# A hybrid attention and RWKV-7 layer: input tiles in rings of four, gated outputs stored as split halves, and the first pair's sums of squares emitted later

## The chip, the cores and the metric

The kernel runs on one core of a Trainium2 chip. The metric is the time of one launch in device microseconds, from three runs. The core has a matrix engine (TensorE, PE in the profile), a vector engine (VectorE, DVE), a scalar engine (ScalarE, ACT), GpSimd (POOL) and a synchronisation engine (SyncE, SP) from whose queue nearly all transfers are issued. Each engine works through its own list of instructions in order; an instruction that needs another engine's result, or a buffer that is still being read, waits for it at the head of its list, and everything behind it on that engine waits too.

## The reference

One layer over a sequence of 256 frames of width 4096. A combined projection feeds sixteen heads of forgetting attention (FoX), 32 heads of an RWKV-7 scan and a SiLU gate; the gated outputs go through an output projection and a layer norm.

```python
proj = jnp.einsum('bsd,dc->bsc', x, w_in)
fox_cols, rw_cols, z = ...
...
fox_out = _fox_attention(fq, fk, fv, log_f)
...
rw = rw + (rw_prev - rw) * mu_shift
r, kr, vr, wd, ad = jnp.split(rw, ...)
w_raw = -jax.nn.softplus(-(w0 + jnp.tanh(wd) @ w_up)) - 0.5
decay = jnp.exp(-jnp.exp(w_raw))
a = jax.nn.sigmoid(a0 + ad @ a_up)
kk = (kr * k_k).reshape(hs)
kk = kk / jnp.maximum(jnp.linalg.norm(kk, axis=-1, keepdims=True), 1e-12)
kr = kr * (1.0 + (a - 1.0) * k_a)
y = _rwkv7_scan(rh, decay, kh, vh, -kk, kk * ah)
y = groupnorm(y) * gn_gain + gn_bias
bonus = jnp.sum(rh * kh * r_k, axis=-1, keepdims=True) * vh
rwkv_out = y + bonus
h = jnp.concatenate([fox_out, rwkv_out], axis=-1) * jax.nn.silu(z)
out = jnp.einsum('bsc,cd->bsd', h, w_out)
x = _layernorm(ALPHA * x + out, ln_gain, ln_bias, LN_EPS)
```

## The kernel before, in words

**Precision.** Every large product is made from split operands. A tile is copied to a rounded type (hi), and the rest, the tile minus hi, is a second tile of that type (lo). ScalarE makes hi (the copies in lines 139, 160 and 744) and VectorE lo (the subtractions in lines 140, 161 and 745). A product is then three matmuls: x hi by w hi (L145), x lo by w hi (L146) and x hi by w lo (L147).

**The prelude.** The 32 k-tiles of the activations (128 x 256 each) come in 17 pieces, two single ones and then pairs. For each piece three transfers are issued: the activations (xr, L112), the narrow LoRA columns (lr, L115; the first three from ScalarE's queue) and the first block's weights (wr, L118, a ring of four). Each xr and each lr has a buffer of its own. Then, per piece, the x tiles are split into x0 to x31, which stay in memory through the projection, lr is split and multiplied (accl), and wr is split and multiplied (acc).

**The main loop.** Eight pairs n of head groups by four blocks b of 512 columns by sixteen weight pieces q. `weights` hands out the next split piece and `fetch` (L216) issues the load of a later one into the ring of four raw buffers, followed by its split, whose hi and lo tiles have three buffers each. A piece is twelve matmuls of 128 x 512. In the timelines w_9h, w_9l are the halves of piece 9 of some block; with a program's numbers w2_0_11l is pair 2, block 0, piece 11. Between the matmuls `slot` advances generators that emit the rest of the work a step at a time: `ahead` (the LoRA products lp and `prepare`, for the head groups i), `chain` (`rwkv` for the pairs), `fox` (attention per head) and `unload`. A `wait(n)` in a generator lets n such steps pass; the table W holds the counts. A compile-time scheduler with a model of durations then sets the order on each engine, so that a changed line can move neighbours too.

**prepare(i)** makes the keys of head group i and, in the tile shl (hi and lo halves of 128 x 512), squares and products whose sums over each head come from two matmuls np with a matrix of ones (L446, L447), `W["np"]`, 6, steps after shl. VectorE goes on from np with n2, a reciprocal, ae and BK.

**rwkv(n)** runs the scan of pair n in chunks. It makes T by way of memory (td, T), transposes T into X on VectorE (L542), and forms qt (L548), Q, xp (L569) from them on TensorE. At its end the group norm runs on the pair's post tile: vs on TensorE, a square root on ScalarE (L626, with a table load ahead of it), a reciprocal (L627), two products and sums (L628, L629), and the gate.

**gate(y, key, k)** (L346) makes h = 0.5 y sz on VectorE (L349), 128 x 256. There are 32 such tiles, two attention and two RWKV ones per pair. Those with k below 28 ("far", the first seven pairs) are stored to the DRAM tensor hd (L351, 128 KB each); the last four stay in memory.

**The reload.** While the last block of the last pair runs, `get_h` (L738) brings the far tiles back for the output projection: `load_h` issues hin from hd, up to three ahead in a ring of three (L735), and get_h splits hin into the buffers of the x tiles, tile h_k in that of x_k, which TensorE must have read for the last time. The output projection (L765 to L767) multiplies the h tiles with the pieces of w_o (wo0_0 and on, from the same stream and ring as the weights), and the layer norm follows.

Of the kernel before, what the change touches and what calls it, by code (L numbers as in the profile page):

```python
# [10 lines left out]
F32 = mybir.dt.float32  # L11
BF16 = mybir.dt.bfloat16
F32R = mybir.dt.float32r
AF = mybir.ActivationFunctionType
ALU = mybir.AluOpType
AX = mybir.AxisListType

P = 128
S = 256
D = 4096  # L20
KT = D // P
G = 16
# [14 lines left out]
INNER = 14  # L37
# [4 lines left out]
W = {"fo": 3, "vs": 2, "np": 6, "gp": 5, "tp": 4, "d1": 8, "d2": 12, "xp": 3, "fs": 4, "fp": 5}  # L42
# [15 lines left out]
LW = 2 * LORA + NF  # L58
# [23 lines left out]
def layer(ctx: ExitStack, tc: tile.TileContext, xt, xtok, w_lora, w_main, w_o, up, par, mulora, fbias, lng, lnb, cst, out):  # L82
    nc = tc.nc
# [3 lines left out]
    dram = ctx.enter_context(tc.tile_pool(name="dram", bufs=1, space=bass.MemoryType.DRAM))  # L87
# [12 lines left out]
    spool = early.enter_context(tc.tile_pool(name="spool", bufs=1))  # L100
# [7 lines left out]
    l_raw = []  # L108
    w_raw = []
    for n, (k0, k1) in enumerate(pieces):  # L110
        raw = spool.tile([P, (k1 - k0) * S], F32, tag=f"xr{n}", name=f"xr{n}")
        nc.sync.dma_start(out=raw, in_=xt[:, k0:k1, :].rearrange("p k t -> p (k t)"))  # L112
        x_raw.append(raw)
        raw = spool.tile([P, (k1 - k0) * LW], F32, tag=f"lr{n}", name=f"lr{n}")
        (nc.scalar if n < 3 else nc.sync).dma_start(out=raw, in_=w_lora[:, k0:k1, :].rearrange("p k c -> p (k c)"))  # L115
        l_raw.append(raw)
        raw = wpool.tile([P, 1024], F32, tag="wr", name=f"wr{n}", bufs=4)
        nc.sync.dma_start(out=raw[:, : (k1 - k0) * OB], in_=w_main[0, 0][:, k0:k1, :].rearrange("p k c -> p (k c)"))  # L118
        w_raw.append(raw)
# [12 lines left out]
    def column(name, i):  # L132
        return prm[:, PAR.index(name), i : i + 1]
# [22 lines left out]
    for n, (k0, k1) in enumerate(pieces):  # L156
        for k in range(k0, k1):
            t = xpool.tile([P, 2, S], F32R, tag=f"x{k}", name=f"x{k}")
# [31 lines left out]
    def wait(n):  # L190
        for _ in range(n):
            yield
# [4 lines left out]
    def slot():  # L197
        for g in list(sides):
            try:
                next(g)  # L200
            except StopIteration:
                sides.remove(g)
# [42 lines left out]
    rp = mid.enter_context(tc.tile_pool(name="rp", bufs=1))  # L245
# [9 lines left out]
    def rt(name):  # L255
        return t256("t", name, 5)
# [18 lines left out]
    lr = const.tile([LORA, 2, 2, S], F32R, name="lr")  # L275
# [58 lines left out]

    hs = {}
    szs = {}
    hd = dram.tile([2 * G, P, S], F32, name="hd")

    def silu2(z, key):
        th = t256("zt", key + "t")  # L340
# [5 lines left out]
    def gate(y, key, k):  # L346
        far = k < 2 * INNER
        h = rp.tile([P, S], F32, tag="h" if far else f"h{k}", name=f"h{k}", bufs=2 if far else 1)
        nc.vector.scalar_tensor_tensor(h, y, 0.5, szs[key], ALU.mult, ALU.mult)  # L349
        if far:  # L350
            nc.sync.dma_start(out=hd[k], in_=h)  # L351
        hs[k] = h

    HALF = [slice(0, C), slice(C, P)]
# [1 line left out]
    def ch(t):  # L356
        return t.rearrange("p (c t) -> p c t", t=C)

    def flat(t):
        return t.rearrange("p a b -> p (a b)")  # L360
# [13 lines left out]
    def front(i):  # L374
        upt = ups[i]
        uph = rp.tile([LORA, 2, P], F32R, tag="uph", name=f"uph{i}")
        nc.scalar.copy(flat(uph), flat(upt))
        upl = rp.tile([LORA, 2, P], F32R, tag="upl", name=f"upl{i}")
        nc.vector.tensor_tensor(flat(upl), flat(upt), flat(uph).bitcast(F32), ALU.subtract)
        load_up(i + 1)  # L380
        yield
        lp = pst(f"lp{i}")
        for j in range(2):
            o = lp[:, j * S : (j + 1) * S]
            nc.tensor.matmul(o, uph[:, j, :], lr[:, j, 0, :], start=True, stop=False)
            nc.tensor.matmul(o, uph[:, j, :], lr[:, j, 1, :], start=False, stop=False)
            nc.tensor.matmul(o, upl[:, j, :], lr[:, j, 0, :], start=False, stop=True)
        tw = rt(f"tw{i}")
        nc.scalar.activation(tw, lp[:, :S], AF.Tanh, scale=0.5, bias=half[:, 0, i : i + 1])
        ta = rt(f"ta{i}")  # L390
        nc.scalar.activation(ta, lp[:, S:], AF.Tanh, scale=0.5, bias=half[:, 1, i : i + 1])
        yield
        nc.vector.tensor_scalar(tw, tw, -0.5 * DECAY, -0.5 * DECAY, ALU.mult, ALU.add)
        L = rt(f"L{i}")
        nc.vector.tensor_tensor_scan(L, cs[:, C_SCAN : C_SCAN + S], tw, 0.0, ALU.mult, ALU.add)
        eL = rp.tile([P, NCH, C + 1], F32, tag="eL", name=f"eL{i}")
        nc.gpsimd.memset(eL[:, :, 0:1], 1.0)
        nc.scalar.activation(eL[:, :, 1:], ch(L), AF.Exp)
        eI = t256("eI", f"eI{i}")
        nc.scalar.activation(eI, L, AF.Exp, scale=-1.0)  # L400
        yield
        am = t256("am", f"am{i}")
        nc.scalar.activation(am, ta, AF.Identity, scale=hka[:, 0, i : i + 1], bias=hka[:, 1, i : i + 1])
        ae = t256("ae", f"ae{i}")
        nc.vector.scalar_tensor_tensor(ae, ta, 1.0, eI, ALU.add, ALU.mult)
        return eL, eI, am, ae
# [3 lines left out]
    def prepare(i):  # L410
        n, u = divmod(i, 2)
        while u == 0 and n and n - 1 not in done:
            yield
        eL, eI, am, ae = yield from front(i)
        while (i, 1) not in rk:
            yield
        r, kr = rk[i, 0], rk[i, 1]
        if u == 0:
            pairs[n] = dict(
                lc=rp.tile([P, 2, NCH], F32, tag="lc", name=f"lc{n}"),  # L420
                BK=rp.tile([P, 2, NCH, P], F32, tag="BK", name=f"BK{n}"),
                lt=[rp.tile([P, 2, NCH, P], F32, tag=f"lt{j}", name=f"lt{j}_{n}") for j in range(2)],
                bon=rp.tile([P, 2, S], F32, tag="bon", name=f"bon{n}"),
            )
        q = pairs[n]
        k = rt(f"k{i}")
        nc.vector.tensor_tensor(k, kr, am, ALU.mult)
        sb = rp.tile([P, 2, S], F32, tag="Nb", name=f"sb{i}")
        nc.scalar.activation(sb[:, 0, :], kr, AF.Square, scale=column("k_k", i))
        nc.vector.scalar_tensor_tensor(sb[:, 1, :], r, column("r_k", i), k, ALU.mult, ALU.mult)  # L430
        shl = rp.tile([P, 2, 2, S], F32R, tag="shl", name=f"shl{i}")
        sh, sl = flat(shl[:, 0]), flat(shl[:, 1])
        nc.scalar.copy(sh, flat(sb))
        nc.vector.tensor_tensor(sl, flat(sb), sh.bitcast(F32), ALU.subtract)
        BK = q["BK"][:, u]
        lt = [q["lt"][j][:, u] for j in range(2)]
        nc.scalar.copy(q["lc"][:, u, :], eL[:, :, C])
        nc.vector.scalar_tensor_tensor(lt[0][:, :, 0:C], ch(kr), nkk[:, i : i + 1], eL[:, :, 0:C], ALU.mult, ALU.mult)
        nc.vector.tensor_tensor(lt[0][:, :, C:P], ch(r), eL[:, :, 1:], ALU.mult)
        nc.scalar.copy(lt[1][HALF[1]], lt[0][HALF[1]])  # L440
        for j in range(2):
            h = HALF[j]
            nc.vector.tensor_tensor(BK[h, :, KB[j][1]], ch(k)[h], ch(eI)[h], ALU.mult)
        yield from wait(W["np"])
        nps = pst(f"np{i}")
        nc.tensor.matmul(nps, onesr, sl, start=True, stop=False)  # L446
        nc.tensor.matmul(nps, onesr, sh, start=False, stop=True)  # L447
        n2 = rt(f"n2{i}")
        nc.vector.tensor_scalar(n2, nps[:, :S], 1e-24, None, ALU.max)
        nc.scalar.copy(q["bon"][:, u, :], nps[:, S:])  # L450
        nc.vector.reciprocal(n2, n2)
        nc.vector.scalar_tensor_tensor(ae, ae, 0.5, n2, ALU.mult, ALU.mult)
        for j in range(2):
            h = HALF[j]
            nc.vector.scalar_tensor_tensor(BK[h, :, KB[j][0]], ch(kr)[h], column("k_k", i)[h], ch(ae)[h], ALU.mult, ALU.mult)
        prepared.add(i)
# [267 lines left out]

    ht = {}

    hin = {}

    def load_h(k):
        if k in hin or k >= 2 * INNER:  # L730
            return
        while k not in hs:
            slot()
        hin[k] = rp.tile([P, S], F32, tag="hin", name=f"hin{k}", bufs=3)
        nc.sync.dma_start(out=hin[k], in_=hd[k])  # L735

    def get_h(k):
        for n in range(k, min(k + 3, 2 * INNER)):  # L738
            load_h(n)
        while k not in hs:  # L740
            slot()
        src = hin.get(k, hs[k])
        t = xpool.tile([P, 2, S], F32R, tag=f"x{k}", name=f"h{k}")
        nc.scalar.copy(t[:, 0, :], src)
        nc.vector.tensor_tensor(t[:, 1, :], src, t[:, 0, :].bitcast(F32), ALU.subtract)
        ht[k] = t

    def load_tok(b):
# [59 lines left out]
    for b, q in outs:  # L808
        if q == 0:
            pool, tag = (ps, "ps") if b == 1 or b and b % 2 == 0 else (pp, "pp")  # L810
# [3 lines left out]
        for j in range(2):  # L814
            k = 2 * q + j
# [138 lines left out]
```

## Time and profile before

| what | us |
|---|---|
| median of three runs | 1998.69 |
| lowest and highest run | 1998.67 and 2004.73 |
| the profiled execution's own time | 2001.74 |
| its span, first to last instruction | 1999.9 |
| TensorE busy in the span | 1977.0 |
| VectorE busy | 1331.2 |
| ScalarE busy | 1001.4 |

The span lies inside the profiled execution's time, and that execution was 3.05 us longer than the median run. The mean clock granted to TensorE was 0.993 of full speed. A row of a timeline gives the start, the duration, the engine, the line and operation, and in brackets how long the engine sat idle before it and what released it. A row of windows gives, for each stretch, the busy microseconds of TensorE, its weight loads, VectorE, ScalarE and GpSimd with the number of instructions, then TensorE's clock, the busy share of the DMA engines and the rate in GB/s.

### The profile page before, as it was taken

The numbers are of one execution on the slowest core, as the hardware profiler recorded it, in microseconds if no ns is written. First come the engines' busy times: TensorE is split into PE (matmuls) and PEld (weight loads), VectorE is DVE, ScalarE is ACT, GpSimd is POOL, SyncE is SP. The second block draws the span as 40 slices with busy tenths as digits, with TensorE's granted clock in tenths as the row PEclk, the third lists the DMA queues.
The fourth block names the chain that finished last, engine by engine and source line by source line (L and its number), as shares of the span: only waits on it lengthen the run. The fifth ranks groups of instructions, "written<-read, shape, count | busy, mean of one in ns | idle before, by whom it ended". The sixth has DMA issues, their size and how long they took to land.

```text
span 1999.9 us, 28369 instructions
## 1 busy us (share of the span) xinstructions
PE 1977.0 (99%) x10624; PEld 1619.1 (81%) x10624; DVE 1331.2 (67%) x2067; ACT 1001.4 (50%) x1506; POOL 34.8 (2%) x82
## 2 busy tenths in 40 slices
PE   8999999999999999999999999999999999999998
PEld 6878888888888888888888887888788878888885
DVE  5578567856785677567757685768576856655555
ACT  5554464456544654465446544644564555433332
POOL 0000000000000000000000000000000000000000
PEclk9999999999999999999999999999999999999998
DMA  8456556655665556555655665566556657866564
GB/s 289 142 187 194 181 169 198 187 188 164 191 194 177 175 180 194 182 181 179 199 172 182 184 206 159 178 194 199 161 170 208 215 182 233 270 192 192 186 201 157
DMA packets 140138, 379.74 MB, mean 190 GB/s; under 512 B 32168, under 2 KB 49592, under 8 KB 140000
## 3 DMA queue, kind: packets, MB, share of 16 engines
q1 hardware_dynamic: 139568, 377.50, 59.7%
q8 instruction: 83, 1.36, 0.3%
q10 hardware_dynamic: 432, 0.43, 0.1%
q14 instruction: 55, 0.45, 0.1%
HBM read 367.89 MB, written 9.98 MB: 189 GB/s over the span
## 4 chain that ended last, share of the span: by engine, by line
PE 92%; DMA 1%; DVE 1%; ACT 0%; SPq 0%; issue 0%; DVEq 0%; ACTq 0%
PE acc L145 22%; PE acc L147 22%; PE acc L146 22%; PE oacc L765 6%; PE oacc L767 6%; PE oacc L766 6%; PE tr L704 1%; PE yp L610 1%; PE gp L470 1%; PE up L585 1%; PE rh L558 1%; DMA hin<-hd 1%; PE sp L594 0%; PE vp L479 0%; DVE res L881 0%; PE tp L515 0%
## 5 line engine op out<-in xcount | busy, mean ns | idle before, releaser
L526 DVE TENSOR_TENSOR prod<-Nb,xc 128x8 f32<-128x8 f32 (+30 forms) x248 | 72.5, 292 | 7.7
L529 DVE TENSOR_REDUCE xc<-prod 128x8 f32<-128x16 f32 (+30 forms) x248 | 73.1, 295 | 6.0
L140 DVE TENSOR_TENSOR w_9l<-w,w_9h 128x1024 fp32r<-128x1024 f32 x31 | 37.9, 1223 | 51.9 <-ACT w_9h L139 50.1
L140 DVE TENSOR_TENSOR w_3l<-w,w_3h 128x1024 fp32r<-128x1024 f32 x31 | 37.9, 1224 | 36.7 <-ACT w_3h L139 36.7
L140 DVE TENSOR_TENSOR w_0l<-w,w_0h 128x1024 fp32r<-128x1024 f32 x31 | 37.9, 1223 | 32.9 <-ACT w_0h L139 32.9
L140 DVE TENSOR_TENSOR w_2l<-w,w_2h 128x1024 fp32r<-128x1024 f32 x31 | 37.9, 1223 | 32.1 <-ACT w_2h L139 32.1
L140 DVE TENSOR_TENSOR w_15l<-w,w_15h 128x1024 fp32r<-128x1024 f32 x31 | 37.9, 1224 | 31.7 <-ACT w_15h L139 31.7
L140 DVE TENSOR_TENSOR w_10l<-w,w_10h 128x1024 fp32r<-128x1024 f32 x31 | 37.9, 1224 | 30.9 <-ACT w_10h L139 30.9
L139 ACT CAST w_15h<-w 128x1024 fp32r<-128x1024 f32 x31 | 32.7, 1055 | 50.9 <-PE acc L146 49.6
L139 ACT CAST w_1h<-w 128x1024 fp32r<-128x1024 f32 x31 | 32.7, 1055 | 49.9 <-PE acc L146 49.9
L139 ACT CAST w_0h<-w 128x1024 fp32r<-128x1024 f32 x31 | 32.7, 1055 | 49.9 <-PE acc L146 49.9
L140 DVE TENSOR_TENSOR w_11l<-w,w_11h 128x1024 fp32r<-128x1024 f32 x31 | 37.6, 1212 | 28.5 <-ACT w_11h L139 28.5
L139 ACT CAST w_14h<-w 128x1024 fp32r<-128x1024 f32 x31 | 32.7, 1055 | 46.8 <-PE acc L146 45.0
L140 DVE TENSOR_TENSOR w_14l<-w,w_14h 128x1024 fp32r<-128x1024 f32 x31 | 37.9, 1223 | 26.8 <-ACT w_14h L139 26.8
L139 ACT CAST w_11h<-w 128x1024 fp32r<-128x1024 f32 x31 | 32.7, 1055 | 45.9 <-PE acc L146 43.8
L140 DVE TENSOR_TENSOR w_1l<-w,w_1h 128x1024 fp32r<-128x1024 f32 x31 | 37.9, 1222 | 22.6 <-ACT w_1h L139 22.4
L145 PE MATMUL acc<-w_4h,x 128*128 128x512 f32 x124 | 53.0, 427 | 0.0
L139 ACT CAST w_13h<-w 128x1024 fp32r<-128x1024 f32 x31 | 32.7, 1055 | 38.4 <-PE acc L146 26.7
L145 PE MATMUL acc<-w_6h,x 128*128 128x512 f32 x124 | 51.2, 413 | 0.0
L145 PE MATMUL acc<-w_1h,x 128*128 128x512 f32 x124 | 51.2, 413 | 0.0
L145 PE MATMUL acc<-w_2h,x 128*128 128x512 f32 x124 | 51.0, 411 | 0.0
L145 PE MATMUL acc<-w_5h,x 128*128 128x512 f32 x124 | 50.0, 403 | 0.0
(800 smaller groups left out, 6538.2 us busy)
## 6 DMA issues: line engine op xcount, KB each, us to landing
w<-in_w_main_dram SPq DMA_DIRECT2D x496, 512.0 KB, 3.5
wo<-in_w_o_dram SPq DMA_DIRECT2D x128, 512.0 KB, 3.5
Nb<-nd SPq DMA_DIRECT2D x16, 512.0 KB, 5.1
wr<-in_w_main_dram SPq DMA_DIRECT2D x15, 512.0 KB, 4.0
res<-in_xtok_dram SPq DMA_DIRECT2D x16, 256.0 KB, 4.4
xr<-in_xt_dram SPq DMA_DIRECT2D x15, 256.0 KB, 5.8
hd<-h SPq DMA_DIRECT2D x28, 128.0 KB, 5.2
hin<-hd SPq DMA_DIRECT2D x28, 128.0 KB, 3.8
```

The lines of the kernel that those rows point to most:

```text
L139: nc.scalar.copy(hi[:, :n], src[:, :n])
L140: nc.vector.tensor_tensor(lo[:, :n], src[:, :n], hi[:, :n].bitcast(F32), ALU.subtract)
L145: nc.tensor.matmul(acc[:, :n], xs[k][:, 0, tt], hi[:, o : o + n], start=(k == 0), stop=False)
L146: nc.tensor.matmul(acc[:, :n], xs[k][:, 1, tt], hi[:, o : o + n], start=False, stop=False)
L147: nc.tensor.matmul(acc[:, :n], xs[k][:, 0, tt], lo[:, o : o + n], start=False, stop=(k == KT - 1))
L470: nc.tensor.matmul(gp[u][j][:, c * P : (c + 1) * P], BK[h, u, c, :], lt[j][h, u, c, :], start=True, stop=True)
L526: first = nc.vector.tensor_tensor(prod[:, :, :, s + 1 :], nb[:, :, s : s + 1, s + 1 :].to_broadcast([P, 2, NJ, w]), xc[:, :, :, s + 1 :], ...
L529: nc.vector.tensor_reduce(xc[:, :, :, s : s + 1], prod[:, :, :, s:], AX.X, ALU.add)
L558: nc.tensor.matmul(rh[HALF[j], u * C : (u + 1) * C], lt[j][:, u, c, 0:C], SV[j][:, u, c, :], start=True, stop=True)
L765: nc.tensor.matmul(acc, ht[k][:, 0, tt], hi[:, o], start=(k == 0), stop=False)
L766: nc.tensor.matmul(acc, ht[k][:, 1, tt], hi[:, o], start=False, stop=False)
L767: nc.tensor.matmul(acc, ht[k][:, 0, tt], lo[:, o], start=False, stop=(k == KT - 1))
```

## The change

Three edits. First, the tiles xr and lr of the prelude get two tags with four buffers each; a piece's load can be issued when the piece four before it has been split. Second, `gate` itself splits a far tile, hl (two buffers), and stores both halves, 256 KB, into hd, which has twice the columns and 28 entries; `get_h` for such a tile is one transfer of 256 KB from hd straight into the x tile's buffer, and `load_h` with its ring is gone. Third, for pair 0 the wait ahead of np is 12 steps in place of 6. No arithmetic is changed: the same copies and subtractions are made in another place.

```diff
-        raw = spool.tile([P, (k1 - k0) * S], F32, tag=f"xr{n}", name=f"xr{n}")
-        nc.sync.dma_start(out=raw, in_=xt[:, k0:k1, :].rearrange("p k t -> p (k t)"))
+        raw = spool.tile([P, 2 * S], F32, tag="xr", name=f"xr{n}", bufs=4)
+        nc.sync.dma_start(out=raw[:, : (k1 - k0) * S], in_=xt[:, k0:k1, :].rearrange("p k t -> p (k t)"))
         x_raw.append(raw)
-        raw = spool.tile([P, (k1 - k0) * LW], F32, tag=f"lr{n}", name=f"lr{n}")
-        (nc.scalar if n < 3 else nc.sync).dma_start(out=raw, in_=w_lora[:, k0:k1, :].rearrange("p k c -> p (k c)"))
+        raw = spool.tile([P, 2 * LW], F32, tag="lr", name=f"lr{n}", bufs=4)
+        (nc.scalar if n < 3 else nc.sync).dma_start(out=raw[:, : (k1 - k0) * LW], in_=w_lora[:, k0:k1, :].rearrange("p k c -> p (k c)"))
...
-    hd = dram.tile([2 * G, P, S], F32, name="hd")
+    hd = dram.tile([2 * INNER, P, 2 * S], F32, name="hd")
...
         if far:
-            nc.sync.dma_start(out=hd[k], in_=h)
+            hl = rp.tile([P, 2, S], F32R, tag="hl", name=f"hl{k}", bufs=2)
+            nc.scalar.copy(hl[:, 0, :], h)
+            nc.vector.tensor_tensor(hl[:, 1, :], h, hl[:, 0, :].bitcast(F32), ALU.subtract)
+            nc.sync.dma_start(out=hd[k], in_=flat(hl).bitcast(F32))
         hs[k] = h
...
-        yield from wait(W["np"])
+        yield from wait(W["np"] if n else 2 * W["np"])
...
-    hin = {}
-
-    def load_h(k):
-        if k in hin or k >= 2 * INNER:
-            return
-        while k not in hs:
-            slot()
-        hin[k] = rp.tile([P, S], F32, tag="hin", name=f"hin{k}", bufs=3)
-        nc.sync.dma_start(out=hin[k], in_=hd[k])
-
     def get_h(k):
-        for n in range(k, min(k + 3, 2 * INNER)):
-            load_h(n)
-        while k not in hs:
-            slot()
-        src = hin.get(k, hs[k])
         t = xpool.tile([P, 2, S], F32R, tag=f"x{k}", name=f"h{k}")
-        nc.scalar.copy(t[:, 0, :], src)
-        nc.vector.tensor_tensor(t[:, 1, :], src, t[:, 0, :].bitcast(F32), ALU.subtract)
+        if k < 2 * INNER:
+            assert k in hs
+            nc.sync.dma_start(out=flat(t).bitcast(F32), in_=hd[k])
+        else:
+            nc.scalar.copy(t[:, 0, :], hs[k])
+            nc.vector.tensor_tensor(t[:, 1, :], hs[k], t[:, 0, :].bitcast(F32), ALU.subtract)
         ht[k] = t
```

**VectorE at the gate of a pair**, in block (2,0), as the program had it before. h6 is the gated attention output, h5 and h7 the two RWKV ones, post1 the group norm's tile, w2_0_10l and on the weights' lo halves, tw4 and L4 the start of a later head group's decay:

```order
L140 TENSOR_TENSOR w2_0_10l_4341<-w2_0_10_4338,w2_0_10h_4340 128x1024
L349 SCALAR_TENSOR_TENSOR h6_4298<-fo3_4296,f3s_4043 128x256
L627 RECIPROCAL post1_4280<-post1_4280 128x512
L140 TENSOR_TENSOR w2_0_11l_4378<-w2_0_11_4375,w2_0_11h_4377 128x1024
L628 TENSOR_TENSOR post1_4280<-post1_4280 128x512
L393 TENSOR_SCALAR tw4_4357<-tw4_4357 128x256
L629 TENSOR_TENSOR post1_4280<-post1_4280,bon1_2766 128x512
L395 SCALAR_TENSOR_TENSOR L4_4368<-cs_72,tw4_4357 128x256
L349 SCALAR_TENSOR_TENSOR h5_4320<-post1_4280,r2s_3596 128x256
L349 SCALAR_TENSOR_TENSOR h7_4323<-post1_4280,r3s_4047 128x256
L140 TENSOR_TENSOR w2_0_12l_4400<-w2_0_12_4397,w2_0_12h_4399 128x1024
```

And with the change, at the same place of VectorE:

```order
L349 SCALAR_TENSOR_TENSOR h6_4313<-fo3_4311,f3s_4058 128x256
L353 TENSOR_TENSOR hl6_4315<-h6_4313,hl6_4315 128x256
L630 RECIPROCAL post1_4295<-post1_4295 128x512
L396 TENSOR_SCALAR tw4_4381<-tw4_4381 128x256
L631 TENSOR_TENSOR post1_4295<-post1_4295 128x512
L398 SCALAR_TENSOR_TENSOR L4_4392<-cs_72,tw4_4381 128x256
L632 TENSOR_TENSOR post1_4295<-post1_4295,bon1_2778 128x512
L140 TENSOR_TENSOR w2_0_11l_4402<-w2_0_11_4399,w2_0_11h_4401 128x1024
L349 SCALAR_TENSOR_TENSOR h5_4338<-post1_4295,r2s_3608 128x256
L349 SCALAR_TENSOR_TENSOR h7_4344<-post1_4295,r3s_4062 128x256
L408 SCALAR_TENSOR_TENSOR ae4_4413<-ta4_4383,eI4_4397 128x256
L353 TENSOR_TENSOR hl5_4340<-h5_4338,hl5_4340 128x256
```

Four instructions that followed w2_0_11l now precede it, and h6's split stands ahead of the reciprocal; the splits of h5 and h7 stand ahead of w2_0_12l. On ScalarE at the same place, with the change:

```order
L139 CAST w2_0_10h_4364<-w2_0_10_4362 128x1024
L673 COPY fo3_4311<-fop3_4308 128x256
L352 CAST hl6_4315<-h6_4313 128x256
L629 ACT_TABLE_LOAD
L629 ACTIVATE post1_4295<-vs1_4331,gneps_829 128x512
L139 CAST w2_0_11h_4401<-w2_0_11_4399 128x1024
```

The cast of hl6 is new there; the others stood in this order before.

**SyncE's queue in the last block**, with the change (h16 and on are reloads, w7_3_12 and on the block's weights, T7 the tiles that X is made of, wo0_0 the first piece of w_o):

```order
L734 DMA h16_14597<-hd_848 128x512
L734 DMA h17_14611<-hd_848 128x512
L734 DMA h18_14619<-hd_848 128x512
L216 DMA w7_3_12_14621<-in_w_main_dram 128x1024
L734 DMA h19_14633<-hd_848 128x512
L734 DMA h20_14641<-hd_848 128x512
L216 DMA w7_3_13_14643<-in_w_main_dram 128x1024
L734 DMA h21_14655<-hd_848 128x512
L734 DMA h22_14663<-hd_848 128x512
L216 DMA w7_3_14_14665<-in_w_main_dram 128x1024
```

Before, w7_3_12 stood behind the load of hin12, and a load waited for its place in the ring of three; now the weight stands behind h18. VectorE at the end of that block before, up to X:

```order
L745 TENSOR_TENSOR h26_14705<-hin26_14677,h26_14705 128x256
L140 TENSOR_TENSOR wo0_2l_14779<-wo0_2_14776,wo0_2h_14778 128x1024
L552 COPY Q7_14750<-qt7_14733 32x256
L745 TENSOR_TENSOR h27_14720<-hin27_14694,h27_14720 128x256
L542 STREAM_TRANSPOSE X_836<-T7_14554 32x8x32 x4
L560 COPY R7_0_14806<-rh7_0_14801 128x128
```

and with the change:

```order
L140 TENSOR_TENSOR w7_3_15l_14690<-w7_3_15_14687,w7_3_15h_14689 128x1024
L140 TENSOR_TENSOR wo0_0l_14712<-wo0_0_14709,wo0_0h_14711 128x1024
L545 STREAM_TRANSPOSE X_836<-T7_14586 32x8x32 x4
L140 TENSOR_TENSOR wo0_1l_14761<-wo0_1_14758,wo0_1h_14760 128x1024
L140 TENSOR_TENSOR wo0_2l_14779<-wo0_2_14776,wo0_2h_14778 128x1024
L575 COPY X_836<-xp7_14782 32x8x32
```

X now follows wo0_0l, and no split of a far h tile is left on this engine.

**VectorE in the first pair**, around np (shl0 and shl1 are the squares of head groups 0 and 1; n20 and BK0 go on from np0), with the change:

```order
L437 TENSOR_TENSOR shl0_1024<-sb0_1021,shl0_1024 128x512
L140 TENSOR_TENSOR w0_1_7l_1090<-w0_1_7_1087,w0_1_7h_1089 128x1024
L140 TENSOR_TENSOR w0_1_8l_1108<-w0_1_8_1105,w0_1_8h_1107 128x1024
L140 TENSOR_TENSOR w0_1_9l_1126<-w0_1_9_1123,w0_1_9h_1125 128x1024
L382 TENSOR_TENSOR upl1_1153<-upt1_919,uph1_1151 96x256
L140 TENSOR_TENSOR w0_1_10l_1160<-w0_1_10_1157,w0_1_10h_1159 128x1024
L452 TENSOR_SCALAR n20_1144<-np0_1141 128x256
L140 TENSOR_TENSOR w0_1_11l_1197<-w0_1_11_1194,w0_1_11h_1196 128x1024
L454 RECIPROCAL n20_1144<-n20_1144 128x256
```

Before, w0_1_9l to w0_1_11l stood behind shl1, some fifteen instructions further on; now they precede the reciprocal of n20. On TensorE np0 moved from piece 6 to behind piece 8, the products lp1 with it, and np1 from piece 9 of this block into the first pieces of the next one.

## The prediction

> **What bounds the kernel now.** I read the page's busy times and slices first, then TensorE's waits, then the clock by windows, and at each wait the timelines of the engines that release it.
>
> ```profile
> PE 1977.0 (99%) x10624; PEld 1619.1 (81%) x10624; DVE 1331.2 (67%) x2067; ACT 1001.4 (50%) x1506; POOL 34.8 (2%) x82
> ...
> PE   8999999999999999999999999999999999999998
> ```
>
> TensorE is busy 1977.0 of 1999.9 us; only the first and the last slice are below 9. The change adds no matmul and takes none away, so it can act only on the gaps and on the clock.
>
> ```profile
> engine line waited for: us in total, times, longest us
> PE xp L569 <- DVE X L542: 3.4, 1, 3.4
> PE acc L145 <- ACT wr5h L139: 2.2, 1, 2.2
> ...
> PE np L446 <- DVE shl L434: 2.0, 1, 2.0
> ...
> PE accl L145 <- ACT wl5h L139: 0.7, 1, 0.7
> ```
>
> Three of these lie where the diff touches: wr5h in the prelude, np in the first pair, xp at the start of the output projection. All the waits together are small, so the forecast is a sum of a few microseconds, and a place that is tight but does not stall today counts as much.
>
> **Prelude.** Rings of four change when the queue of SyncE may issue each xr and lr. The windows (PE and other engines' busy us, then clock, DMA share, GB/s):
>
> ```profile
> 24.00:28.00 4.00, 3.12 (x17) 2.27 (x15) 2.55 (x7) 1.92 (x6) 0.00 (x0) 1.00 1.03 376
> 28.00:32.00 4.00, 1.81 (x9) 1.03 (x7) 1.89 (x3) 2.65 (x7) 0.00 (x0) 0.81 0.93 345
> 32.00:36.00 4.00, 3.96 (x10) 3.10 (x10) 2.61 (x8) 1.49 (x5) 0.00 (x0) 0.50 0.74 230
> ```
>
> The DMA engines are full (share 1.03), so wr5 comes when the bytes queued ahead of it are through. Counting sizes along both SP orders, 9.20 MB stood ahead and 9.04 MB do now: 0.16 MB at 376 GB/s is 0.4 us. But on ScalarE the cast of wr5h goes behind one more pair of x casts (0.71 us in the timeline):
>
> ```profile
> 29.19 0.71 ACT L160 CAST x<-xr 128x256 fp32r<-128x256 f32 x2 [1.73 <-DMA xr<-in_xt_dram]
> 29.80 1.04 ACT L139 CAST wr5h<-wr 128x1024 fp32r<-128x1024 f32 x1
> ```
>
> Those casts wait for their own xr, which is one of the pieces now sent earlier. I take −0.2; the bounds are −1 (half of the 2.2 us stall gone) and +1 (a pair of casts with its wait, 0.71 plus 0.3). Behind it the clock spell at 0.50 stays either way.
>
> **First pair.** The np matmuls go six slots later.
>
> ```profile
> 111.88 0.39 PE L145 MATMUL acc<-w_9h,x 128*128 128x512 f32 x1
> ...
> 119.41 0.39 PE L145 MATMUL acc<-w_10h,x 128*128 128x512 f32 x1
> ```
> ```profile
> 114.07 0.69 DVE L434 TENSOR_TENSOR shl<-sb,shl 128x512 fp32r<-128x512 f32 x1
> ```
> ```profile
> 116.00:120.00 4.00, 4.00 (x11) 3.20 (x12) 4.00 (x5) 0.66 (x1) 0.00 (x0) 0.59 0.73 219
> ```
>
> From w_9 to w_10 TensorE ran 12 matmuls and two of np, 14 of 0.228 us (the cadence 111.88, 112.11, 112.33 of the timeline), 3.2 us, and took 7.53: 4.3 us were lost, 1.96 idle on shl, 0.33 on the w_9l queued behind it, the rest at a clock of 0.59. In the new order np1 stands in the next block, far behind its shl1, and VectorE makes w_9l, w_10l and w_11l ahead of the second head group's work. By adding up these rows' durations along the new VectorE order, w_12l, the last piece behind that work, ends at about 119.7, and TensorE, no longer late, asks for it at 120.2. So the loss goes but for a restart: −4.2, bounds −4.3 and −3.0 (w_12l a microsecond late).
>
> **The gate, seven times.** Every pair but the last gates its outputs while pieces 10 to 12 of a block run. Before:
>
> ```profile
> 463.73 0.42 DVE L349 SCALAR_TENSOR_TENSOR h<-fo,f3s 128x256 f32<-128x256 f32 x1
> 464.96 3.35 DVE L627 RECIPROCAL post<-post 128x512 f32<-128x512 f32 x1 [0.82 <-ACT post L626]
> 468.23 1.20 DVE L140 TENSOR_TENSOR w_11l<-w,w_11h 128x1024 fp32r<-128x1024 f32 x1
> 469.36 0.78 DVE L628 TENSOR_TENSOR post<-post 128x512 f32<-128x512 f32 x1
> ...
> 470.86 0.68 DVE L395 TENSOR_TENSOR_SCAN L<-cs,tw 128x256 f32<-128x256 f32 x1
> 471.46 0.39 DVE L349 SCALAR_TENSOR_TENSOR h<-post,r2s 128x256 f32<-128x256 f32 x1
> ```
> ```profile
> 462.46 0.37 ACT L670 COPY fo<-fop 128x256 f32<-128x256 f32 x1
> 462.84 1.28 ACT L626 ACT_TABLE_LOAD   x1
> 464.24 0.69 ACT L626 ACTIVATE post<-vs,gneps 128x512 f32<-128x512 f32 x1
> ```
> ```profile
> 472.05 0.39 PE L147 MATMUL acc<-w_11l,x 128*128 128x512 f32 x1
> ```
>
> The split's two instructions cost what they cost when the reload did them:
>
> ```profile
> L744 ACT CAST h<-hin x28: 395/406/408, 1571.7 to 1621.6; 128x256 fp32r<-128x256 f32 x28
> L745 DVE TENSOR_TENSOR h<-hin,h x28: 408/420/426, 1573.1 to 1622.1; 128x256 fp32r<-128x256 f32 x28
> ```
>
> Three of the four splits lie in slack. The one of the fox output does not: on ScalarE its cast stands between fo and the table load of the square root, and it must wait for h (ends 464.15). So cast to 464.6, table load 1.28 to 465.85, square root to 466.55: 1.6 us later than 464.93. The reciprocal runs 466.6 to 469.9. And four instructions that stood behind w_11l now stand ahead of it: L628, tw, L629 and the scan, by their starts 471.46 − 469.36 = 2.10 us. So w_11l starts at 472.0 and ends at 473.2. TensorE's order puts its use two matmuls later, at 472.05 + 0.46 = 472.51: a stall of 0.7. Behind it w_12l, with two splits ahead of it now, ends at about 475.8, just as TensorE, 0.7 late itself, asks for it. 7 × 0.7 = **+4.9**. Bounds: 0 (the scan's 0.6 overlapping or the cast arriving early) and +8 (w_12l late by 0.4 as well); below nothing is excluded, since nothing idles there before.
>
> **The last block and the start of the projection.** The wait for xp:
>
> ```profile
> 1616.10 5.50 DMA hin<-hd
> ...
> 1622.06 0.43 DVE h L745
> 1622.48 0.34 DVE X L542
> ```
> ```profile
> 1620.00:1624.00 4.00, 0.63 (x12) 0.51 (x11) 1.89 (x5) 1.35 (x2) 0.00 (x0) 1.00 0.83 306
> 1624.00:1628.00 4.00, 4.00 (x44) 3.38 (x43) 2.13 (x4) 1.01 (x3) 0.00 (x0) 0.57 0.30 74
> ```
>
> X stood on VectorE behind the split of h27, and that behind a load issued at 1616.10. Now there is no split, X follows wo0_0l with no h ahead of it, and qt runs ahead of piece 12. The idle 3.37 and 4 × (1 − 0.57) = 1.7 of slow clock go: **−5.1**; low bound −3.4, if the slow spell stayed.
>
> In exchange 28 reloads of 256 KB instead of 128 KB share the queue with the weights, and each waits until TensorE has read its x tile for the last time. Weight 12 now stands behind h18, hence behind the last use of x18:
>
> ```profile
> 1597.73 0.39 PE L147 MATMUL acc<-w_9l,x 128*128 128x512 f32 x1
> ...
> 1605.21 0.39 PE L147 MATMUL acc<-w_12l,x 128*128 128x512 f32 x1
> ```
> ```profile
> 1590.92 0.33 SPq L216 DMA_DIRECT2D w<-in_w_main_dram  x1
> ```
> ```profile
> w<-in_w_main_dram SPq DMA_DIRECT2D x5, 512.0 KB, 3.9
> ```
>
> So it is issued at about 1598.6 and not at 1590.92. It is used at about 1606.3 (two matmuls and the small ones of qt, 0.6 us in the timeline, later than 1605.21), less cast and subtract, 1.05 + 1.22 + gaps: it must land by 1603.95, 5.35 us after issue. Landings took 3.9 in 1588 to 1625, with half the reload bytes. Per piece of 2.73 us (12 × 0.228) now 1.05 MB move, 384 GB/s. The nearest rates of full DMA engines:
>
> ```profile
> 16.00:20.00 4.00, 3.47 (x21) 2.73 (x20) 3.20 (x6) 2.25 (x5) 0.00 (x0) 1.00 1.05 389
> ...
> 1592.00:1596.00 4.00, 4.00 (x20) 3.33 (x20) 3.19 (x6) 2.35 (x6) 0.00 (x0) 1.00 0.97 298
> ```
>
> At 389 GB/s there is no loss; at 298/0.97 = 307 a piece takes 3.42 us, 0.69 over, and over the eleven pieces 5 to 15 that is 7.6 less what the ring has in hand. The reload's rows are now 2 KB, as xr's in the prelude, so I go near the fast end: **+1.2**, bounds 0 and +7.
>
> The Trainium skill, DMA: Bandwidth & Descriptors, "Specifications", puts the limit of one core's HBM traffic at about 358 GB/s. The prelude's windows, at 389 and 376, lie above it. By that figure a piece would take 2.93 us, 0.20 over, and the term would be at most 11 × 0.20 = +2.2, an estimate.
>
> Elsewhere the 28 doubled stores are spread over 1400 us and lie beside matmuls.
>
> **Sum.** −0.2 − 4.2 + 4.9 − 5.1 + 1.2 = −3.4 us. The profiled execution took 2001.74 us around its span of 1999.9; the median run took 1998.69, so the saving is taken from the median: 1998.69 − 3.4 = **1995.3**. About 0.3%, 6.0 us, is what this measurement tells from no change.
>
> **Rivals.**
> - The gate stalls stay hidden, because ScalarE's table load does not wait or the scan is not ahead. For it: only 0.7 us decides. Against: every row of the chain is there. −8.3, 1990.4. Chance 0.17.
> - The reload becomes the bound of the last block: it decides once a weight lands over 5.35 us after issue, and then each piece costs up to 0.69. For it: 307 GB/s in this very block. Against: that was 1 KB rows. +7.6 in place of +1.2: +3.0, 2001.7, slower than before though little. Chance 0.15.
> - The gate stalls slow the clock. After 2.0 us on shl it fell to 0.59 and cost 2.0 more; the 0.7 us on wl5h, in 24 to 28, left it at 1.00. It decides from a stall between these. At 0.59 four microseconds lose 1.6; 7 × 1.6 = +11.2: +7.8, 2006.5. Chance 0.12.
> - The slow clock at np and xp isn't the stalls' doing and stays: they give back their idle alone, 2.3 and 3.4. −0.2 − 2.3 + 4.9 − 3.4 + 1.2 = +0.2, 1998.9. Chance 0.05.
> - The later np doesn't rid TensorE of the wait, VectorE being full there whatever the order: that term 0, +0.8, 1999.5. Chance 0.06.
>
> The fourth is what the Trainium skill, TensorE: Matmul & The Clock Gate, "Why this matters for your kernels", would give: there only gaps over about 3 us slow the clock. Here a gap of 2.0 us did, so the trace speaks against it.
>
> **Numbers.** My forecast has 0.45, its own range 1991.5 to 1999. Faster by over 0.3% (under 1992.7): the first rival's 0.17 and 0.13 of the forecast's lower end, 0.30. Slower (over 2004.7): the clock's 0.12 and 0.06 of the reload's upper end, 0.18. The rest 0.52. The range, 1989.5 to 2003.5, takes in the first two rivals and leaves out the clock.
>
> **What would show it.** np's wait and xp's wait gone, windows there at clock 1.00 (wrong if another wait of 2 us follows). At 471 to 474 and six times more, a wait of TensorE for w_11l of 0.5 to 0.9 us. In 1598 to 1616, weights landing 4 to 6 us after issue, and waits for wh or wl of w_12 to wo_0 adding up to 1 to 2 us. The forecast is wrong if these waits sum to over 5, if w_11l is not waited for, or if the clock falls behind it.

## The result, and the profile after

Over 20 runs each, the changed kernel took 2002.54 us in the median and the kernel before 2001.32. The ratio of the two is 1.0005, with a 95% interval of 0.9998 to 1.0012: no difference that can be told. The profiled execution's span is 2000.3 us, 0.4 over that of before. That small number is the sum of large ones, as TensorE's waits show (what waited, for what, microseconds in total, times, longest):

```profile
PE acc L147 <- DVE w_11l L140: 2.9, 7, 0.4
PE zp L864 <- DVE z L858: 2.1, 1, 2.1
PE acc L145 <- ACT w_12h L139: 2.0, 1, 2.0
PE acc L145 <- ACT wr5h L139: 1.8, 1, 1.8
...
PE acc L147 <- DVE wr6l L140: 1.2, 1, 1.2
```

The waits for xp (3.4) and np (2.0) are gone. In their place stand seven waits for w_11l, one for w_12h of 2.0, and a longer one for wr6l.

To see what each place is worth, I compare when TensorE starts the same matmul in the two traces. In the kernel before, these are the first matmuls of block (0,1), of pair 1, and of the last block (7,3), and of the third piece of the output projection:

```profile
83.18 0.39 PE L145 MATMUL acc<-w_0h,x 128*128 128x512 f32 x1
...
230.96 0.50 PE L145 MATMUL acc<-w_0h,x 128*128 128x512 f32 x1
...
1569.42 0.39 PE L145 MATMUL acc<-w_0h,x 128*128 128x512 f32 x1
...
1630.58 0.50 PE L765 MATMUL oacc<-wo_2h,h 128*128 128x512 f32 x1
```

And in the changed kernel:

```profile
82.23 0.39 PE L145 MATMUL acc<-w_0h,x 128*128 128x512 f32 x1
...
225.92 0.50 PE L145 MATMUL acc<-w_0h,x 128*128 128x512 f32 x1
...
1570.11 0.39 PE L145 MATMUL acc<-w_0h,x 128*128 128x512 f32 x1
...
1630.37 0.50 PE L757 MATMUL oacc<-wo_2h,h 128*128 128x512 f32 x1
```

The offset is −0.95, then −5.04, then +0.69, then −0.21. Its steps are the price of each stage; a last step of +0.6 lies behind that, in the tail of the span. No edit touches the rest of the projection or the layer norm there, and the executions of the experiments below show 0.0 to 1.1.

| stage | forecast | measured |
|---|---|---|
| prelude, to block (0,1) | −0.2 | −0.95 |
| pair 0 | −4.2 | −4.09 |
| seven gates, to the last block | +4.9 | +5.73 |
| last block and start of the projection | −5.1 + 1.2 = −3.9 | −0.90 |
| rest of the span | 0 | +0.6 |
| sum | −3.4 | +0.4 |

**A gate after the change**, on ScalarE, VectorE and TensorE:

```profile
458.20 0.37 ACT L673 COPY fo<-fop 128x256 f32<-128x256 f32 x1
459.92 0.41 ACT L352 CAST hl<-h 128x256 fp32r<-128x256 f32 x1 [1.35 <-DVE h L349]
460.34 1.28 ACT L629 ACT_TABLE_LOAD   x1
461.64 0.69 ACT L629 ACTIVATE post<-vs,gneps 128x512 f32<-128x512 f32 x1
```
```profile
458.33 1.23 DVE L140 TENSOR_TENSOR w_10l<-w,w_10h 128x1024 fp32r<-128x1024 f32 x1 [1.10 <-ACT w_10h L139]
...
462.36 3.35 DVE L630 RECIPROCAL post<-post 128x512 f32<-128x512 f32 x1 [1.58 <-ACT post L629]
...
467.55 1.22 DVE L140 TENSOR_TENSOR w_11l<-w,w_11h 128x1024 fp32r<-128x1024 f32 x1
```
```profile
468.82 0.73 PE L147 MATMUL acc<-w_11l,x 128*128 128x512 f32 x2 [0.41 <-DVE w_11l L140]
```

ScalarE stood still for 1.35 us behind fo, waiting for h, with the table load queued behind it; VectorE then waited 1.58 us for the square root. The whole kernel runs about four microseconds ahead here, so times are read against w_10l, which before the change stood here:

```profile
462.58 1.23 DVE L140 TENSOR_TENSOR w_10l<-w,w_10h 128x1024 fp32r<-128x1024 f32 x1 [1.10 <-ACT w_10h L139]
```

From its start to the reciprocal's it was 2.38 us then and is 4.03 now.

**The last block after the change.** SyncE's issues, ScalarE's cast, and windows (busy us of the five engines, clock, DMA share, GB/s):

```profile
1595.28 3.80 SPq L540 DMA_DIRECT2D T<-td  x8
1599.18 1.32 SPq L734 DMA_DIRECT2D h<-hd  x3
1600.60 0.38 SPq L216 DMA_DIRECT2D w<-in_w_main_dram  x1
```
```profile
1607.15 1.04 ACT L139 CAST w_12h<-w 128x1024 fp32r<-128x1024 f32 x1 [8.69 <-DMA w<-in_w_main_dram]
```
```profile
1596.00:1600.00 4.00, 4.00 (x19) 3.31 (x18) 1.73 (x3) 1.05 (x1) 0.00 (x0) 1.00 0.50 141
1600.00:1604.00 4.00, 4.00 (x19) 3.32 (x18) 0.00 (x0) 0.00 (x0) 0.00 (x0) 1.00 0.83 232
1604.00:1608.00 4.00, 2.24 (x40) 1.58 (x38) 0.00 (x0) 0.84 (x1) 0.00 (x0) 1.00 0.96 366
1608.00:1612.00 4.00, 3.75 (x10) 2.99 (x11) 2.81 (x3) 1.61 (x3) 0.00 (x0) 0.58 0.81 314
```

Weight 12 was issued at 1600.60, behind eight loads of T and three reloads, and landed 6.5 us later. TensorE waited 2.0 us and then ran at a clock of 0.58. The DMA engines were at half in 1596 to 1600, just before the issue: until then the weight was not waiting for them but for its turn in the queue. After it they were at 0.83 and 0.96, busy with the reloads too, and weights took long to land. These rows give the weights issued in 1560 to 1605, with the median time to landing at the end, before:

```profile
w<-in_w_main_dram SPq DMA_DIRECT2D x14, 512.0 KB, 3.6
```

and with the change:

```profile
w<-in_w_main_dram SPq DMA_DIRECT2D x13, 512.0 KB, 6.4
```

### The profile page after: what moved, and what is told of

It is laid out like the page before. It is cut to its first block, busy times and chain, and to the rows that moved or that the text cites. A ratio compares the mean times of both kernels' runs of the same rounds, so it can differ in the third digit from the quotient of the medians.

```text
span 2000.3 us, 28396 instructions
## 1 busy us (share of the span) xinstructions
PE 1976.9 (99%) x10624; PEld 1615.3 (81%) x10624; DVE 1331.0 (67%) x2067; ACT 1001.2 (50%) x1506; POOL 33.5 (2%) x82
## 4 chain that ended last, share of the span: by engine, by line
PE 92%; DVE 4%; DMA 2%; ACT 1%; issue 1%; SPq 0%; DVEq 0%; ACTq 0%
PE acc L145 22%; PE acc L147 22%; PE acc L146 22%; PE oacc L757 6%; PE oacc L758 6%; PE oacc L759 6%; PE tr L707 1%; DVE post L630 1%; DMA xr<-in_xt_dram 1%; PE yp L613 1%; PE gp L473 1%; PE up L588 1%; PE rh L561 1%; PE sp L597 0%; ACT L629 0%
## 5 line engine op out<-in xcount | busy, mean ns | idle before, releaser
L139 ACT CAST w_10h<-w 128x1024 fp32r<-128x1024 f32 x31 | 32.6, 1050 | 37.5 <-PE acc L146 29.0
L145 PE MATMUL acc<-w_12h,x 128*128 128x512 f32 x124 | 49.1, 396 | 2.0 <-ACT w_12h L139 2.0
L147 PE MATMUL acc<-w_11l,x 128*128 128x512 f32 x124 | 47.9, 396 | 2.9 <-DVE w_11l L140 2.9
```

The lines of the kernel that those rows point to most:

```text
L139: nc.scalar.copy(hi[:, :n], src[:, :n])
L145: nc.tensor.matmul(acc[:, :n], xs[k][:, 0, tt], hi[:, o : o + n], start=(k == 0), stop=False)
L147: nc.tensor.matmul(acc[:, :n], xs[k][:, 0, tt], lo[:, o : o + n], start=False, stop=(k == KT - 1))
```

## The experiments

Each run's time is compared with runs of the kernel before on the same chip, and its trace stage by stage with the one trace of the kernel before that is used above. The stages' offsets come from one profiled execution each, the ratio from all runs; 0.001 of it is 2 us, so that the two agree only to a microsecond or two:

| kernel | prelude | pair 0 | gates | last block | span | ratio, 95% interval |
|---|---|---|---|---|---|---|
| the change | −0.95 | −4.09 | +5.73 | −0.90 | +0.4 | 1.0005 [0.9998, 1.0012] |
| rings and np only | +0.29 | −4.12 | +0.03 | −0.64 | −4.4 | 0.9978 [0.9968, 0.9987] |
| split and reload only | +0.32 | −0.08 | +5.65 | −0.66 | +5.3 | 1.0014 [1.0004, 1.0023] |
| hi copy on GpSimd | −0.54 | −4.14 | +0.09 | −2.31 | −6.3 | 0.9962 [0.9949, 0.9975] |
| last T on GpSimd's queue | −0.52 | −4.14 | +5.69 | −4.63 | −2.5 | 0.9984 [0.9974, 0.9993] |
| both of these | +0.01 | −4.11 | +0.12 | −4.15 | −7.1 | 0.9961 [0.9946, 0.9976] |
| hi copy and reloads on GpSimd | −0.56 | −4.11 | +0.11 | −5.01 | −9.4 | 0.9959 [0.9944, 0.9973] |
| hi copy, T and ones on GpSimd | −0.87 | −4.11 | +0.09 | −4.18 | −8.0 | 0.9957 [0.9943, 0.9972] |
| hi copy, reloads and ones on GpSimd | −2.05 | −4.12 | −0.01 | −4.93 | −10.9 | 0.9949 [0.9936, 0.9963] |

### Rings and the later np alone

The kernel before with the first and the third edit:

```diff
+        raw = spool.tile([P, 2 * S], F32, tag="xr", name=f"xr{n}", bufs=4)
...
+        raw = spool.tile([P, 2 * LW], F32, tag="lr", name=f"lr{n}", bufs=4)
...
+        yield from wait(W["np"] if n else 2 * W["np"])
```

> The kernel before with the rings of four and the later np of pair 0, without the split in the gate and the new reload. Theory (the parts add): the prelude gives 0.95 us and the first pair 4.1, block (0,2)'s start comes 5.0 us earlier and that stays to the end of the span: 5.0 us off, ratio 0.9975; gates as before, xp still waits 3.4 us. Rival (the later np only moves the wait on, or the rings' gain is the luck of one execution): under 3 us off at the second pair, ratio above 0.9985.

Measured: ratio 0.9978 [0.9968, 0.9987], span 4.4 us shorter. Pair 0 gave 4.12, and it stayed to the end; the prelude gave nothing in this execution. The wait for xp remained:

```profile
PE xp L569 <- DVE X L542: 2.8, 1, 2.8
```

The slow clock behind it did not. The wait lies at 1617.4 to 1620.2, and the windows around it show 1.00, where the 3.4 us before had 0.57 behind them:

```profile
1616.00:1620.00 4.00, 1.41 (x7) 0.83 (x5) 2.41 (x5) 1.94 (x3) 0.80 (x2) 1.00 0.93 293
1620.00:1624.00 4.00, 3.77 (x57) 2.98 (x57) 2.90 (x6) 1.23 (x4) 0.00 (x0) 1.00 0.66 213
```

A new wait of 0.9 us, for ScalarE's copy bk (L797), took back part of that, so that the last block gave only 0.64. The np edit is worth what was forecast, and it does not move the wait on. The rings' share can't be told from one execution; that is taken up below.

### The split in the gate and the reload alone

```diff
+            hl = rp.tile([P, 2, S], F32R, tag="hl", name=f"hl{k}", bufs=2)
+            nc.scalar.copy(hl[:, 0, :], h)
+            nc.vector.tensor_tensor(hl[:, 1, :], h, hl[:, 0, :].bitcast(F32), ALU.subtract)
+            nc.sync.dma_start(out=hd[k], in_=flat(hl).bitcast(F32))
...
+            nc.sync.dma_start(out=flat(t).bitcast(F32), in_=hd[k])
```

> The kernel before with the split in the gate and the new reload alone. Theory: each of seven gates costs 0.7 to 0.8 us (w_11l), 5.7 in all; the last block gives back 5.1 at xp and loses 4.2 at w_12: span 4.8 us longer, ratio 1.0024. Rival (the losses after the first pair come from the changed start, that is from the rings and np shifting everything, not from the split): gates under 0.2 us each, ratio within 0.0007 of 1.

Measured: ratio 1.0014 [1.0004, 1.0023], span 5.3 us longer; the interval takes in 1.0023 but not 1.0024. TensorE's waits:

```profile
PE acc L147 <- DVE w_11l L140: 2.9, 7, 0.4
...
PE np L449 <- DVE shl L437: 2.0, 1, 2.0
PE acc L145 <- ACT w_12h L139: 1.9, 1, 1.9
```

Without the rings and the later np the same seven waits for w_11l and the same wait for w_12h stand there, 0.81 us per gate (5.65 / 7). They are this edit's own, and not a result of the changed start. The profiled execution is the slowest of its ten: the ratio makes the loss some 2.8 us and not 5.3. The parts add within the noise: in the spans −4.4 and +5.3 make +0.9, against +0.4 of the change, and the prelude differs by more than that from one execution to the next; in the ratios −0.22% and +0.14% make −0.08%, against +0.05%, and each of the three is known to about 0.1%.

### The gate's hi copy on GpSimd

```diff
-            nc.scalar.copy(hl[:, 0, :], h)
+            nc.gpsimd.tensor_copy(hl[:, 0, :], h)
```

> The changed kernel with the hi copy of the gate's split on GpSimd, so that ScalarE's table load follows the fox output's copy at once; VectorE keeps all its subtractions. Theory (ScalarE's cast behind h delays the square root by 1.6 us): the reciprocal starts 1.6 us earlier against w_10l, the gate costs under 0.2 us per pair, 5 us off the changed kernel, ratio to before 0.9975 to 0.998. Rival (VectorE's four added subtractions, 1.7 us per pair, are what makes w_11l and w_12l late): still 0.5 us or more per pair, ratio 0.9995 to 1.001.

Measured: ratio 0.9962 [0.9949, 0.9975]; the seven gates cost 0.09 us together. GpSimd's copy and VectorE at the place of the change:

```profile
459.59 0.40 POOL L352 CAST hl<-h 128x256 fp32r<-128x256 f32 x1 [4.66 <-issue]
```
```profile
457.91 1.23 DVE L140 TENSOR_TENSOR w_10l<-w,w_10h 128x1024 fp32r<-128x1024 f32 x1 [1.10 <-ACT w_10h L139]
...
460.36 3.35 DVE L630 RECIPROCAL post<-post 128x512 f32<-128x512 f32 x1
463.62 1.16 DVE L140 TENSOR_TENSOR w_11l<-w,w_11h 128x1024 fp32r<-128x1024 f32 x1
```

From w_10l to the reciprocal it is 2.45 us again, and the compile-time scheduler, which now sees the square root in time, puts w_11l back behind the reciprocal. VectorE still makes all four subtractions. So its 1.7 us per gate were in slack, as forecast, and the cast on ScalarE, ahead of the table load, made the stall: by its delay and by the order that followed from it. These two were not tried apart.

The last block also cost less here: its wait for w_12h is 0.8 in place of 2.0, though nothing in it was edited, and the clock stayed at 1.00 behind it. The weight was issued 0.3 us earlier, counted from the start of the block; that this is the reason was not tried.

### The last T on GpSimd's queue

```diff
-                nc.sync.dma_start(out=T[B * a : B * (a + 1), u], in_=td[u, a].rearrange("c r s -> r c s"))
+                (nc.gpsimd if n == G // 2 - 1 else nc.sync).dma_start(out=T[B * a : B * (a + 1), u], in_=td[u, a].rearrange("c r s -> r c s"))
```

> The changed kernel with the eight last loads of T issued from GpSimd's queue; the reloads stay on SyncE's queue with the same bytes. Theory A (SyncE's queue is what makes w_12 late: eight issues of T and three reloads that wait for x16 to x18 stand ahead of it): w_12 is issued before 1597 on the clock of the changed kernel, TensorE's wait for w_12h of 2.0 us and the slow clock behind it are gone, 3 to 4 us off the changed kernel's span, ratio to before 0.9985. Theory B (the DMA engines are full with twice the reload bytes, 384 GB/s needed): weights still land over 6 us after issue, waits of over 1.5 us for weights remain, ratio within 0.0007 of the changed kernel's.

Measured: ratio 0.9984 [0.9974, 0.9993]; the last block gives 4.63 in place of 0.90. Of SyncE's queue:

```profile
1594.83 0.38 SPq L216 DMA_DIRECT2D w<-in_w_main_dram  x1
1596.46 3.04 SPq L734 DMA_DIRECT2D h<-hd  x3
```

The weight issued at 1594.83 is w_12: the scheduler put it ahead of the reloads of x16 to x18 as well. No wait for a weight is left in this block, with the same bytes to move, and the median landing in 1560 to 1605 is 4.0 us, where the change had 6.4. This bears out the queue and speaks against the DMA rate. It does not part the two things that changed in the queue, T's eight issues and the three reloads that now stand behind the weight.

### Both, and all reloads on GpSimd's queue

The edits of the two runs above together:

> The changed kernel with both repairs: the gate's hi copy on GpSimd and the eight last loads of T on GpSimd's queue. Theory (the two losses are separate): gates under 0.1 us per pair, no wait for w_12h, block (0,1) to the end 9 to 9.5 us ahead of the kernel before, ratio 0.9953 (0.994 to 0.9965). Rival (with the gates repaired the last block comes earlier against the transfers and the wait for weights returns, or GpSimd's queue delays T because its hi copies stand ahead): not over 7 us ahead, ratio above 0.9965.

Measured: ratio 0.9961 [0.9946, 0.9976], span 7.1 us shorter. The gates stay repaired and no weight is waited for, but the sum falls short of the 9 forecast. A new small wait took part of it:

```profile
1616.36 0.69 PE L572 MATMUL xp<-X,Q 32*32 32x32 f32 x30 [0.79 <-DVE Q L555]
```

Here the copy of Q that xp needs stands on VectorE behind wo0_1l. The rest is the tail of this execution, 1.0 us longer than in the kernel before.

Then the hi copy and the reloads, with T on SyncE's queue as in the change:

```diff
-            nc.sync.dma_start(out=flat(t).bitcast(F32), in_=hd[k])
+            nc.gpsimd.dma_start(out=flat(t).bitcast(F32), in_=hd[k])
```

> The changed kernel with the gate's hi copy and all 28 reloads on GpSimd's queue, so that no weight stands behind a reload; the bytes of the last block are the same. Theory A (the order of SyncE's queue): the weights of the last block are issued as their ring comes free, no wait for them, 9 to 10 us ahead of the kernel before, ratio 0.995. Theory B (the DMA engines cannot carry 1.05 MB per piece): weights land late all the same, and waits for weights of over 2 us stand in the last block, ratio above 0.9965.

Measured: ratio 0.9959 [0.9944, 0.9973], span 9.4 us shorter; the last block gives 5.01, the whole of xp's loss. Its windows:

```profile
1592.00:1596.00 4.00, 4.00 (x19) 3.30 (x19) 0.26 (x1) 0.43 (x1) 0.54 (x1) 1.00 0.97 362
...
1604.00:1608.00 4.00, 4.00 (x19) 3.34 (x18) 2.38 (x3) 1.75 (x3) 2.98 (x6) 1.00 1.00 355
```
```profile
w<-in_w_main_dram SPq DMA_DIRECT2D x13, 512.0 KB, 4.9
h<-hd POOLq DMA_DIRECT2D x25, 256.0 KB, 4.9
```

The DMA engines are as good as full (0.97 and 1.00), at 362 and 355 GB/s, and weights take 4.9 us to land, longer than the 3.6 before the change and shorter than the 6.4 with it. Nobody waits for one, though T's eight issues are still on SyncE's queue. So moving either, T or the reloads, is enough. A full DMA and late weights are not the same thing: here the first was there without the second, which in the change came from the order of issue.

### The ones on GpSimd

With rings, TensorE waits for wr6l. VectorE in the changed kernel:

```profile
36.97 0.23 DVE L186 CAST onesr<-cs 128x128 fp32r<-128x128 f32 x1 [0.67 <-DMA cs<-in_cst_dram]
37.11 1.22 DVE L140 TENSOR_TENSOR wr6l<-wr,wr6h 128x1024 fp32r<-128x1024 f32 x1
```

The copy of the ones waits for the load of the constants, and wr6l stands behind it; before the change wr6l came first. The edit, on top of the run with the hi copy and T on GpSimd:

```diff
-    nc.vector.tensor_copy(onesr, ones)
+    nc.gpsimd.tensor_copy(onesr, ones)
```

> As the kernel with both repairs, and the matrix of ones is copied on GpSimd, so that wr6l on VectorE no longer stands behind a copy that waits for the constants' load. Theory: TensorE's wait for wr6l (0.9 to 1.9 us in the runs with rings, 0.3 before) falls under 0.4 us, 0.8 to 1.5 us off, ratio to before 0.0005 lower than with both repairs. Rival (wr6l waits for its own cast, the load of the constants being there anyway): no difference, wait for wr6l stays.

Measured: the wait for wr6l, 1.6 in the run without this edit, is no longer among TensorE's waits, and block (0,1) starts 0.88 us earlier than there. The ratio, 0.9957 [0.9943, 0.9972], is 0.0004 lower than that run's, which these intervals can't tell from nothing. The mechanism is shown by the trace, its worth in the time is not.

### Rings, np, and three things on GpSimd

> Rings, later np, the gate's hi copy, all reloads and the copy of the ones on GpSimd. Theory (the losses add): block (0,1) 0.6 to 0.9 us ahead of the kernel before, first pair 4.1, gates 0, xp 5.0: 9.7 to 10.2 us ahead at the end, span 1989.7 to 1990.5, ratio 0.9950 (0.9945 to 0.9958). Rival (what the start gains the transfers behind it take back): not below the run with both on GpSimd, ratio 0.9958 or more.

Measured, in five rounds: 1991.92 us in the median against 2001.76 of the kernel before, ratio 0.9949 [0.9936, 0.9963]. This is the fastest kernel of the study, about half a per cent under the kernel before. Its span, 1989.0, is 0.7 below the forecast's low end: the prelude gave 2.05, more than the 0.6 to 0.9 expected, and 1.2 more than in the run above with the same edits there. The half per cent is shown; that last microsecond may be this execution's luck.

## Why the prediction was right, and where it was off

The forecast was "no change that can be told" as the likeliest case, at 1995.3 us, 3.4 under the median known then. The measured median lies inside the range, and the ratio is 1. In part this is luck. The forecast's own narrower range, 1991.5 to 1999, was missed, and 2002.54 is one microsecond below the upper end of the range: the gates cost 0.8 more than forecast and the reload 3.0, the prelude gave 0.75 more and the tail took 0.6. The 20 runs also put the kernel before at 2001.32 and not at 1998.69, so that the offset is what counts: −3.4 forecast, +0.4 in the profiled spans, about +1 in the medians.

- **Prelude.** −0.2 forecast with bounds of 1 to either side, −0.95 measured; over the six executions that have the rings without the ones on GpSimd it ranges from −0.95 to +0.29, and without rings there are 0 and +0.32. So the rings' share, some half microsecond on average, is less than one execution can show, and it stays open. The wait for wr6l behind the constants was not forecast. Nor does the slow clock behind wr5h stay "either way": in 36 to 40 it is 0.83 before, 1.00 with the change and 0.86 in the run with T and the ones on GpSimd, so that it too varies.
- **Pair 0.** −4.2 against −4.09 to −4.14 in every run that has the edit, with the mechanism as told: no wait for np or w_9l, and the clock at 1.00 throughout:

```profile
112.00:116.00 4.00, 4.00 (x22) 3.36 (x21) 3.95 (x8) 3.39 (x8) 0.00 (x0) 1.00 0.70 245
116.00:120.00 4.00, 4.00 (x19) 3.11 (x18) 3.95 (x9) 3.08 (x4) 0.11 (x1) 1.00 0.00 0
```

- **The gates.** 0.7 each forecast, 0.81 or 0.82 measured. By the starts of its first matmuls piece 11 took 3.43 us and piece 12 2.82 where twelve matmuls take 2.72: 0.71 and 0.10 (the waits' 0.41 counts only the time in which TensorE stood idle). The chain was right in place and size, 1.6 us late at the reciprocal, and the run with GpSimd's copy confirms its first link. The rival that the stall stays hidden fell; so did the one that these stalls slow the clock, which stayed at 1.00:

```profile
468.00:472.00 4.00, 3.58 (x16) 2.50 (x15) 4.00 (x8) 2.75 (x5) 0.00 (x0) 1.00 0.49 157
```

- **xp.** −5.1 forecast. With all reloads on GpSimd's queue no wait is left in the block and it gives 5.01, so the term was right.
- **The reload.** This is the step that failed, in size. The forecast was +1.2; the change lost 5.1 − 0.9 = 4.2: 2.0 us of waiting for w_12h, some 1.5 of slow clock behind it (0.50 in 1608.0 to 1611.3), which was in no term of the sum, and smaller delays. The forecast had w_12 "issued at about 1598.6", from the last use of x18 alone, and then asked how fast the DMA engines are. It left out what stands just ahead of those reloads in SyncE's new order, eight issues of T, 3.80 us of the queue. The block starts 0.7 us later with the change, so its 1598.6 is 1599.3 here; the weight went at 1600.60, 1.3 us after that. It then took 6.5 us to land where the forecast allowed 5.35, another 1.2. The mechanism, a weight landing over that limit, was the rival's, and the forecast's own sign of being wrong, another wait of 2 us, came true; but the price came from one weight and the slow clock behind it, not from 0.69 us on each of eleven pieces. The runs with GpSimd's queues settle that: same bytes, no wait.
- **The slow clock.** The Trainium skill, TensorE: Matmul & The Clock Gate, "Why this matters for your kernels", names gaps over about 3 us. Here the 2.0 us at w_12h brought 0.58, as the 2.0 us at np had brought 0.59 before. The trace differs from the page, and the rival that hung on it fell with pair 0's full −4.1. But the forecast's reading, that a stall somewhere between 0.7 and 2.0 us is enough, does not hold either: 2.8 us at xp, in the run with rings and np only, left the clock at 1.00. The length of the gap alone does not decide.

## What to carry to other kernels

Price an in-order queue by everything that stands ahead of the instruction in question, its own issue times included, before asking how fast the transfers are; a load that waits for a buffer is better off in a queue in which nothing on the critical path stands behind it, as the reloads on GpSimd's queue show. A small operation that waits for another engine is dear where a long chain is queued behind it: 0.41 us of cast, seven times, cost 5.7 us on ScalarE and 0.1 us on an idle engine. When a change of several parts shows no difference, compare the start of the same matmul stage by stage before calling it neutral: here −5 and +6 lay in it.

## What the runs showed of the hardware

GpSimd's copy of 128 x 256 with the rounding took 0.40 us while VectorE was idle, the same as ScalarE's 0.41. Beside a VectorE subtraction both were slower: two copies took 1.86 us, and w_12l 1.41 in place of 1.21.

```profile
467.26 1.86 POOL L352 CAST hl<-h 128x256 fp32r<-128x256 f32 x2 [2.33 <-DVE h L349]
```
```profile
467.45 1.41 DVE L140 TENSOR_TENSOR w_12l<-w,w_12h 128x1024 fp32r<-128x1024 f32 x1
```

An idle gap of TensorE of 2.0 us brought about 3 us of slow clock, at np before and at w_12h with the change; gaps of 0.4, 0.8 and 1.25 us brought none in their windows. But neither did 1.9 us for wr6l in the run with the hi copy on GpSimd (1.00 in 36 to 40), nor 2.8 us for xp with rings and np only. In the trace of the kernel before, the clock records of the slow spells begin at 30.51, 115.85 and 1624.54 us and last 6.83, 3.41 and 3.41. The distances, 85.34 and 1508.69, are 25 and 442 times 3.4133, and the lengths twice and once that. This suggests that the clock is set anew at fixed steps of 3.4 us, so that a gap counts by where it falls; no run here tried it.
